# A two-layer hybrid decoder on one core: the MLP norm's factor is squared and applied behind the second product, and ScalarE's Relu reads the up stage's bank

## The chip, the core and the metric

The kernel runs on one core of one Trainium2 chip. The metric is device microseconds of an execution. A core has five engines with queues of their own: TensorE (PE) multiplies matrices into the banks of PSUM; VectorE (DVE), ScalarE (ACT) and GpSimd (POOL) work element by element; SyncE (SP) issues most of the transfers. Each engine executes its queue in order and waits at the head of it for semaphores of the others.

## The reference, cut to what matters

The reference is a decoder of two layers on 256 tokens of width 1024. Layer A has differential attention, layer B block attention; both also attend into a fixed memory. Each layer ends with an MLP of width 4096 behind an RMS norm:

```python
def _rmsnorm(x, g):
    y = xf * lax.rsqrt(jnp.mean(xf * xf, axis=-1, keepdims=True) + EPS)
    return (y * g.astype(jnp.float32)).astype(x.dtype)

def _sq_relu_mlp(h, w_up, w_down):
    u = jax.nn.relu(h @ w_up)
    return (u * u) @ w_down

x = x + _sq_relu_mlp(_rmsnorm(x, a_norm_mlp[i]), a_w_up[i], a_w_down[i])
```

The norm has one positive factor r per token. The up product is linear in it, relu keeps a positive factor, the square squares it, and the down product is linear again: the factor can be taken out of the whole MLP as r squared, which is 1 / (mean + EPS), without a root.

## The kernel before

Every float32 product is made of three products of rounded parts: high by high, low by high, high by low. Of a weight chunk (128x1024) that a transfer brings, ACT makes the high part (L336) and DVE the low part (L338); there are six buffers of each part, four for the raw chunk. Of a normalized activation ACT makes the high part (L352) and DVE the low one (L354); they carry the gain of the norm but not its factor.

An MLP has two stages. The **up stage** (`mlp_up`) has 16 steps, each of two chunks into one bank `acc` of 128x512: 128 hidden units by 256 tokens, twice. Tokens lie along the free axis there, so the factor is needed as a row repeated over all partitions. PE first sums the squares (L460), DVE makes 1 / sqrt of them in eleven small instructions (L466, the lines of `rsqrt`, L468), multiplies the identity by each half's column (L477), PE multiplies this by ones (L479), and DVE copies the result into `rb` (L481). Then DVE reads each bank as max(bank, 0) times `rb` (L790), ACT squares it (L793), ACT and DVE split it into two parts (L805, L807); for six of the 16 steps DVE also makes four block sums (L800 to L803). There are four `acc` banks and two buffers `u`.

The **down stage** (`natural_down`) turns this around: the hidden activations are the weights of PE, and the result has tokens on partitions, in four banks `t` (half of the tokens by half of the columns). Twelve of the 32 row blocks of the down weights go through a scheme of seven products in place of eight; its extra sums go into four `acc` banks `more`, which `gather` folds into the tiles `ys` (first MLP) or `xs` (last MLP, where they hold the residual stream). In the first MLP DVE then adds each bank `t` to its `ys` (L982), PE transposes (L990) and DVE adds the result to `xT` (L751). In `mlp_last` DVE adds the pieces straight into `xs` (L1027, L1045, L1067), then the final norm follows.

The order of the work is not written out by hand. Every step is given to a planner (`Plan`) with an engine, an assumed duration, what it reads and writes and a priority; `order` runs a list schedule on these costs with the buffers' limits, and the instructions are emitted in the order of the planned starts. So a changed step can move others on its engine.

Of the kernel before, what the change touches and what calls it, by code (L numbers as in the profile page):

```python
# [13 lines left out]
AF = mybir.ActivationFunctionType  # L14
# [5 lines left out]
EPS = 1e-6  # L20
# [205 lines left out]
def tile_hybrid(ctx: ExitStack, tc: tile.TileContext, xa, xb, memt, xnat, mnat, w0, wall, consts, fgain, out):  # L226
# [21 lines left out]
    def bank(cls):  # L248
        return buf(cls, [128, 512], F32, psum)
# [8 lines left out]
    def fixed(shape, nm, dt=F32):  # L258
        return const.tile(shape, dt, name=name(nm))
# [11 lines left out]
    nlam = fixed([128, 1], "nlam")  # L271
    rb_t = fixed([128, S], "rb")
    ppx = fixed([128, 2, 512], "ppx")
# [139 lines left out]
    class Stats:  # L413
# [40 lines left out]

        def rstd(self):
            ps = bank("t")
# [7 lines left out]
            def emit():  # L464
# [3 lines left out]
                nc.vector.tensor_scalar_mul(self.r8, self.r, 0.125)  # L468
            P.add(("dve", 2100, emit), [ps], [self.key])
            return self  # L470

    def bcast(st):

        ps = bank("t")
        for h in range(2):
            dg = buf("dg", [128, 128])
            P.add(("dve", 196, lambda dg=dg, h=h: nc.vector.tensor_scalar_mul(dg.t, ident, st.r[:, h:h + 1])),  # L477
                  [st.key], [dg])
            P.add(("pe", 213, lambda dg=dg, h=h: nc.tensor.matmul(  # L479
                ps.t[:, h * 128:(h + 1) * 128], ones, dg.t, start=True, stop=True)), [dg], [ps])  # L480
        P.add(("dve", t_dve(S), lambda: nc.vector.tensor_copy(rb_t, ps.t[:, 0:S])), [ps], ["rb"])  # L481

# [291 lines left out]
    def mlp_up(st, sums=()):  # L774

        st.rstd()
        us = [big(i, [128, 4, 2, S], F32R) for i in range(8)]
        st_["pieces"] = 1
        first = True
        for b in range(16):  # L780
            u = buf("u", [128, 2, S])
            ps = bank("acc")
            for mi in range(2):
                wh, wl = chunk()
                up_chunk(ps, mi, wh, wl)
            if first:
                bcast(st)
                first = False
            k0 = 2 * b % 4
            P.add(("dve", t_dve(512, True), lambda u=u, ps=ps: nc.vector.scalar_tensor_tensor(  # L790
                u.t, ps.t.rearrange("p (a s) -> p a s", a=2), 0.0, rb_t[:, None, :].to_broadcast([128, 2, S]),
                op0=OP.max, op1=OP.mult)), [ps, "rb"], [u])
            P.add(("act", t_act(512), lambda u=u: nc.scalar.activation(u.t, u.t, AF.Square)), [u], [u])  # L793
# [158 lines left out]
    def mlp(st, done):  # L952
# [4 lines left out]
        def gather(more):  # L957
# [8 lines left out]
            add((1, 1), (1, 0), r5)  # L966
            add((0, 1), (0, 1), r5)

        part = 24
        _, product, u_ = natural_down(us, pss, part, part, gather,  # L970
                                      wsum, lambda a: [("wsum", a)], 4)
        for c in range(2):
# [7 lines left out]
            for hf in range(2):  # L980
                y, ps = ys[hf, c], pss[hf, c]
                P.add(("dve", t_dve(512), lambda y=y, ps=ps: nc.vector.tensor_add(y.t, y.t, ps.t)), [y, ps], [y])  # L982
            for b in range(2):
# [14 lines left out]
    def mlp_last(st):  # L998
# [22 lines left out]
        def gather(more):  # L1021
# [7 lines left out]
            def to(cell, src, key, port=False):  # L1029
                x = xs[cell]  # L1030
                add(lambda: x.t, lambda: x.t, src, [(x, 0), (x, 1), key], [(x, 0), (x, 1)], port)
            r1, r5, r6, r7 = more
# [11 lines left out]
        x, ps, tail = xs[1, 1], pss[1, 1], bank("acc")  # L1044
        P.add(("dve", t_dve(S), lambda x=x, ps=ps: nc.vector.tensor_add(x.t[:, S:], x.t[:, S:], ps.t[:, S:])),  # L1045
              [ps, (x, 1)], [(x, 1)])
        for hf in range(2):
            ss, part_, r = fixed([128, 4], "ss"), fixed([128, 1], "part"), fixed([128, 1], "rstd")
            for c in range(2):
# [5 lines left out]
                for i in range(2):  # L1055
# [4 lines left out]
                    if c == 1 and i == 1:  # L1060
# [5 lines left out]
                    dump = buf("sq", [128, S])  # L1066
                    P.add(("dve", t_dve(S), lambda x=x, ps=ps, sl=sl: nc.vector.tensor_add(  # L1067
                        x.t[:, sl], x.t[:, sl], ps.t[:, sl])), [ps, (x, i)], [(x, i)])
                    P.add(("act", t_act(S) + 100, lambda x=x, sl=sl, dump=dump, ss=ss, j=2 * c + i: nc.scalar.activation(
# [332 lines left out]
```

## Time and profile before

| what | value |
|---|---|
| time, median of three runs | 599.97 us (599.6 to 600.78) |
| span of the profiled execution | 725.8 us |
| mean clock granted to TensorE in it | 0.755 |
| PE busy | 716.6 us |
| DVE busy | 491.3 us |
| ACT busy | 398.0 us |
| POOL busy | 54.4 us |
| moved by transfers | 108.45 MB, mean 149 GB/s |

The profiled execution took longer than the timed ones; its page gives the span and no time around it. In the views "<-" behind an idle time names what ended it, and a group's line gives the line of the kernel, the engine, the operation, what it writes and reads, the number of instructions, the busy time and the mean duration. PEld is the loading of PE's weights, which overlaps the products. One product of float32 parts in the source can stand as several records.

### The profile page before, as it was taken

How to read it: one execution, taken by the hardware profiler on the slowest of the kernel's cores; microseconds unless marked ns; L12 is line 12 of the kernel's file. 1: busy time of each engine (PE TensorE's matmuls, PEld its weight loads, DVE VectorE, ACT ScalarE, POOL GpSimd, SP SyncE). 2: the span in 40 equal slices, each digit the busy share in tenths (PEclk: the TensorE clock that was granted, in tenths of full speed). 3: DMA queues.
4: the chain of work that ended last, by engine and by line, in shares of the span. 5: the costliest groups of instructions: out<-in, count | busy, mean ns of one | idle time of the engine just before them, and what ended most of it. 6: DMA issues, size and time to landing. Idle time of an engine off the chain costs nothing.

```text
span 725.8 us, 10368 instructions
## 1 busy us (share of the span) xinstructions
PE 716.6 (99%) x3794; PEld 590.5 (81%) x3794; DVE 491.3 (68%) x871; ACT 398.0 (55%) x750; POOL 54.4 (8%) x67
## 2 busy tenths in 40 slices
PE   9999999999999999999999999999999999999996
PEld 7676769999999977677777776889999999776775
DVE  5777666587556687766776577675675666876664
ACT  6776666455544554444575477656464455554422
POOL 0121110030000000000111121001200000000002
PEclk8777777777777777777777777777777777777777
DMA  8854432435444433546455432224444443354421
GB/s 303 293 183 165 146 95 79 145 119 175 151 168 146 152 139 132 188 145 209 139 174 179 169 120 85 88 88 143 153 164 152 154 158 125 127 186 151 148 85 59
DMA packets 30003, 108.45 MB, mean 149 GB/s; under 512 B 3328, under 2 KB 3328, under 8 KB 29696
## 3 DMA queue, kind: packets, MB, share of 16 engines
q1 hardware_dynamic: 29664, 107.26, 43.4%
q8 instruction: 30, 0.49, 0.3%
q10 hardware_dynamic: 288, 0.52, 0.2%
q14 instruction: 21, 0.17, 0.1%
HBM read 106.72 MB, written 1.05 MB: 148 GB/s over the span
## 4 chain that ended last, share of the span: by engine, by line
PE 98%; DVE 1%; DMA 1%; ACT 0%; issue 0%; SPq 0%; ACTq 0%
PE acc L821 30%; PE acc L499 23%; PE t L871 23%; PE acc L765 7%; PE acc L871 6%; PE t L586 2%; PE t L624 2%; PE t L681 1%; PE t L557 1%; DMA xT<-xa 1%; PE t L1013 0%; PE t L990 0%; DVE xT L751 0%; PE t L579 0%; PE t L721 0%; PE t L720 0%
## 5 line engine op out<-in xcount | busy, mean ns | idle before, releaser
L336 ACT CAST wh<-w 128x512 fp32r<-128x512 f32 (+1 forms) x232 | 182.5, 814 | 191.3 <-PE acc L821 74.0
L338 DVE TENSOR_TENSOR wl<-w,wh 128x512 fp32r<-128x512 f32 (+1 forms) x232 | 213.4, 939 | 86.7 <-ACT wh L336 71.7
L821 PE MATMUL acc<-xn,wh 128*128 128x256 f32 x1024 | 157.3, 314 | 0.5 <-DVE xn L354 0.5
L821 PEld LDWEIGHTS acc<-xn,wh 128*128 128x128 f32 x1024 | 150.7, 224 | 0.7 <-DVE xn L354 0.7
L871 PE MATMUL t<-wh,B 128*128 128x512 f32 (+1 forms) x368 | 134.4, 453 | 0.0
L499 PE MATMUL acc<-wh,xn 128*128 128x512 f32 x256 | 101.6, 472 | 0.7 <-ACT xn L352 0.7
L871 PEld LDWEIGHTS t<-wh,B 128*128 128x128 f32 x368 | 72.5, 199 | 29.8
L821 PE MATMUL acc<-xn,wl 128*128 128x256 f32 x512 | 84.1, 314 | 0.0
L871 PE MATMUL t<-wl,B 128*128 128x512 f32 (+1 forms) x184 | 82.9, 450 | 0.0
L821 PEld LDWEIGHTS acc<-xn,wl 128*128 128x128 f32 x512 | 78.1, 224 | 0.0
L499 PEld LDWEIGHTS acc<-wh,xn 128*128 128x128 f32 x256 | 51.0, 199 | 23.5 <-issue 2.2
L765 PE MATMUL acc<-B,wh 128*128 128x256 f32 x256 | 60.1, 323 | 0.0
L499 PE MATMUL acc<-wl,xn 128*128 128x512 f32 x128 | 58.0, 453 | 0.0
L790 DVE SCALAR_TENSOR_TENSOR u<-acc,rb 128x512 f32<-128x512 f32 x32 | 21.9, 690 | 50.5 <-PE acc L821 50.5
L871 PEld LDWEIGHTS t<-wl,B 128*128 128x128 f32 x184 | 37.0, 201 | 15.1
L765 PEld LDWEIGHTS acc<-B,wh 128*128 128x128 f32 x256 | 46.3, 216 | 0.9 <-issue 0.8
L452 POOL TENSOR_TENSOR sqa<-sqa,sq 128x256 f32<-128x256 f32 x21 | 20.3, 966 | 295.7 <-ACT sq L451 294.9
L765 PE MATMUL acc<-B,wl 128*128 128x256 f32 x128 | 40.0, 313 | 0.0
L895 DVE TENSOR_TENSOR wl<-wsum,wh 128x1024 fp32r<-128x1024 f32 x24 | 29.4, 1223 | 8.9 <-ACT wh L894 6.5
L533 POOL TENSOR_TENSOR ropet<-ropes,consts 128x256 f32<-128x256 f32 (+1 forms) x28 | 25.1, 917 | 129.0 <-ACT ropes L522 106.5
L499 PEld LDWEIGHTS acc<-wl,xn 128*128 128x128 f32 x128 | 26.8, 210 | 9.1
L894 ACT CAST wh<-wsum 128x1024 fp32r<-128x1024 f32 x24 | 25.3, 1052 | 15.9 <-PE acc L871 6.9
(223 smaller groups left out, 899.1 us busy)
## 6 DMA issues: line engine op xcount, KB each, us to landing
w<-wall SPq DMA_DIRECT2D x191, 512.0 KB, 3.3
w<-memt SPq DMA_DIRECT2D x4, 512.0 KB, 5.0
B<-xnat SPq DMA_DIRECT2D x1, 1024.0 KB, 7.4
B<-mnat SPq DMA_DIRECT2D x1, 1024.0 KB, 8.9
xT<-xa SPq DMA_DIRECT2D x1, 540.0 KB, 3.8
w<-w SPq DMA_DIRECT2D x2, 256.0 KB, 3.5
xT<-xb SPq DMA_DIRECT2D x1, 512.0 KB, 6.6
consts<-consts SPq DMA_DIRECT2D x1, 256.5 KB, 4.5
```

The source lines that it names most:

```text
L336: P.add(("act", t_act(n), lambda sl=sl: nc.scalar.copy(h.t[:, sl], w.t[:, sl])), [(w, x) for x in q], [(h, x) for x in q])
L338: P.add(("dve", t_dve(n), lambda sl=sl: nc.vector.tensor_sub(l.t[:, sl], w.t[:, sl], h.t[:, sl].bitcast(F32))), [(w, x) for x in q] + [(h, ...
L452: P.add(("pool", t_pool(S), lambda: nc.gpsimd.tensor_tensor(self.acc.t, self.acc.t, sq.t, op=OP.add)), [sq, self.acc], [self.acc])
L499: nc.tensor.matmul(pss[hf].t[:, c0:c1], a(k)[:, ts], b.t[:, o + c0:o + c1], start=(k == 0 and i == 0), stop=(k == KT - 1 and i == 2))
L533: nc.gpsimd.tensor_tensor(t.t[:, 0:nh, e:e + 32], zs.t[:, 0:nh, 32 - e:64 - e], b(sin[:, e:e + 32]), op=OP.mult)
L586: nc.tensor.matmul(sp[hd].t[:, c], qk[a].t[r, qb * 128:(qb + 1) * 128], qk[b].t[r, S:S + c.stop - c.start], start=(qb == 0 and i == 0 and ...
L765: nc.tensor.matmul(o, a.t[:, ws], x(k), start=(n == 0 and m % 2 == 0 and i == 0), stop=(n == KT - 1 and i == 2), skip_group_check=True)
L790: P.add(("dve", t_dve(512, True), lambda u=u, ps=ps: nc.vector.scalar_tensor_tensor(u.t, ps.t.rearrange("p (a s) -> p a s", a=2), 0.0, rb_ ...
L821: nc.tensor.matmul(ps.t[:, o], w.t[:, k * 128:(k + 1) * 128], xnt[:, k, x], skip_group_check=True, **flags)
L871: nc.tensor.matmul(ps.t[:, c0:c1], x, y, start=start and i == 0, stop=stop and i == 2, skip_group_check=True)
L894: P.add(("act", t_act(m), lambda: nc.scalar.copy(h[x].t[:, :m], src())), keys, [h[x]])
L895: P.add(("dve", t_dve(m), lambda: nc.vector.tensor_sub(l[x].t[:, :m], src(), h[x].t[:, :m].bitcast(F32))), keys + [h[x]], [l[x]], port=True)
```

## The change

The factor is no longer applied to the up stage's bank. `rstd(True)` makes r squared with two instructions, a multiply-add and a reciprocal; `bcast` and `rb` are gone. ACT reads the bank with Relu. Behind the down product the factor is a column, one number per token's partition: in the first MLP ACT scales the four gathered `ys`, and DVE's sum of bank and `ys` becomes a multiply-add; in the last MLP each sum into the residual tiles becomes a multiply-add with the column.

```diff
-        def rstd(self):
+        def rstd(self, squared=False):
...
-            P.add(("dve", 2100, emit), [ps], [self.key])
+            def square():
+                ms = fixed([128, 2], "ms")
+                nc.vector.tensor_scalar(ms, ps.t[:, 0:2], 1.0 / D, EPS, op0=OP.mult, op1=OP.add)
+                nc.vector.reciprocal(self.r, ms)
+            P.add(("dve", 350, square) if squared else ("dve", 2100, emit), [ps], [self.key])
...
-    def bcast(st):
-        ps = bank("t")
-        for h in range(2):
-            dg = buf("dg", [128, 128])
-            P.add(("dve", 196, lambda dg=dg, h=h: nc.vector.tensor_scalar_mul(dg.t, ident, st.r[:, h:h + 1])),
-                  [st.key], [dg])
-            P.add(("pe", 213, lambda dg=dg, h=h: nc.tensor.matmul(
-                ps.t[:, h * 128:(h + 1) * 128], ones, dg.t, start=True, stop=True)), [dg], [ps])
-        P.add(("dve", t_dve(S), lambda: nc.vector.tensor_copy(rb_t, ps.t[:, 0:S])), [ps], ["rb"])
...
     def mlp_up(st, sums=()):
-        st.rstd()
+        st.rstd(True)
...
-            P.add(("dve", t_dve(512, True), lambda u=u, ps=ps: nc.vector.scalar_tensor_tensor(
-                u.t, ps.t.rearrange("p (a s) -> p a s", a=2), 0.0, rb_t[:, None, :].to_broadcast([128, 2, S]),
-                op0=OP.max, op1=OP.mult)), [ps, "rb"], [u])
+            P.add(("act", t_act(512, True), lambda u=u, ps=ps: nc.scalar.activation(
+                u.t, ps.t.rearrange("p (a s) -> p a s", a=2), AF.Relu)), [ps], [u])
...
             add((0, 1), (0, 1), r5)
+            for (hf, c), y in ys.items():
+                P.add(("act", t_act(512, False, True), lambda y=y, hf=hf: nc.scalar.activation(
+                    y.t, y.t, AF.Copy, scale=st.r[:, hf:hf + 1])), [y, st.key], [y])
...
-                P.add(("dve", t_dve(512), lambda y=y, ps=ps: nc.vector.tensor_add(y.t, y.t, ps.t)), [y, ps], [y])
+                P.add(("dve", t_dve(512), lambda y=y, ps=ps, hf=hf: nc.vector.scalar_tensor_tensor(
+                    y.t, ps.t, st.r[:, hf:hf + 1], y.t, op0=OP.mult, op1=OP.add)), [y, ps, st.key], [y])
...
-                add(lambda: x.t, lambda: x.t, src, [(x, 0), (x, 1), key], [(x, 0), (x, 1)], port)
+                P.add(("dve", t_dve(512), lambda: nc.vector.scalar_tensor_tensor(
+                    x.t, src(), st.r[:, cell[0]:cell[0] + 1], x.t, op0=OP.mult, op1=OP.add)),
+                    [(x, 0), (x, 1), key, st.key], [(x, 0), (x, 1)], port=port)
...
-                    P.add(("dve", t_dve(S), lambda x=x, ps=ps, sl=sl: nc.vector.tensor_add(
-                        x.t[:, sl], x.t[:, sl], ps.t[:, sl])), [ps, (x, i)], [(x, i)])
+                    P.add(("dve", t_dve(S), lambda x=x, ps=ps, sl=sl, hf=hf: nc.vector.scalar_tensor_tensor(
+                        x.t[:, sl], ps.t[:, sl], st.r[:, hf:hf + 1], x.t[:, sl], op0=OP.mult, op1=OP.add)),
+                        [ps, (x, i), st.key], [(x, i)])
```

The step at L1045 is changed in the same way. The planner makes a new order of this. SP's and POOL's rows stand as before. On PE the only difference in the whole program is four rows. The place is the start of the first MLP's up stage, before; `acc_...` are banks, `xn` the activations, `wh` and `wl` the parts of a chunk, `sqa` the sums of squares, `dg` the diagonals:

```order
L460 MATMUL t_1742<-ones_116,sqa_1596 128x1 x2
L821 MATMUL acc_1615<-xn_67,wl_1515 128x256 x4
L821 MATMUL acc_1615<-xn_67,wh_1538 128x256 x16
L821 MATMUL acc_1615<-xn_67,wl_1546 128x256 x8
L821 MATMUL acc_1625<-xn_67,wh_1568 128x256 x2
L821 MATMUL acc_1625<-xn_67,wl_1635 128x256 x8
L479 MATMUL t_1813<-dg_1805,ones_116 128x128
L479 MATMUL t_1813<-dg_1807,ones_116 128x128
L821 MATMUL acc_1625<-xn_67,wh_1612 128x256 x16
```

The same place after the change, where the line of `up_chunk` is L809:

```order
L460 MATMUL t_1741<-ones_115,sqa_1595 128x1 x2
L809 MATMUL acc_1614<-xn_67,wl_1514 128x256 x4
L809 MATMUL acc_1614<-xn_67,wh_1537 128x256 x16
L809 MATMUL acc_1614<-xn_67,wl_1545 128x256 x8
L809 MATMUL acc_1624<-xn_67,wh_1567 128x256 x2
L809 MATMUL acc_1624<-xn_67,wl_1634 128x256 x8
L809 MATMUL acc_1624<-xn_67,wh_1611 128x256 x16
```

The two rows L479 are gone and nothing else has moved; the second MLP's up stage loses its two in the same way.

On ACT the same up stage begins like this before (L336 casts a chunk, L793 squares, L805 makes the high part):

```order
L336 CAST wh_1724<-w_1560 128x1024
L336 CAST wh_1738<-w_1641 128x1024
L336 CAST wh_1785<-w_1707 128x1024
L336 CAST wh_1799<-w_1730 128x1024
L336 CAST wh_1841<-w_1767 128x1024
L793 ACTIVATE u_1843<-u_1843 128x512
L805 CAST B_394_1867<-u_1843 128x2x256
L793 ACTIVATE u_1854<-u_1854 128x512
L805 CAST B_394_1867<-u_1854 128x2x256
```

And after (L335 is the cast of a chunk, L779 the Relu, L781 the square, L793 the high part):

```order
L335 CAST wh_1723<-w_1559 128x1024
L779 ACTIVATE u_1737<-acc_1598 128x512
L335 CAST wh_1744<-w_1640 128x1024
L781 ACTIVATE u_1737<-u_1737 128x512
L793 CAST B_377_1768<-u_1737 128x2x256
L335 CAST wh_1783<-w_1706 128x1024
L779 ACTIVATE u_1795<-acc_1614 128x512
L335 CAST wh_1803<-w_1729 128x1024
L781 ACTIVATE u_1795<-u_1795 128x512
L793 CAST B_377_1768<-u_1795 128x2x256
```

The first bank is read before four of the casts that used to stand ahead of its square, and a Relu that waits for PE stands in front of casts.

Near the end of the first MLP's down stage ACT's order is this before (L963 copies the first gathered sum, L352 makes parts of the memory's activations):

```order
L963 COPY qh_3221<-acc_2799 128x512
L336 CAST wh_3228<-w_3173 128x1024
L336 CAST wh_3233<-w_3185 128x1024
L336 CAST wh_3245<-w_3211 128x1024
L336 CAST wh_3269<-w_3235 128x1024
L336 CAST wh_3283<-w_3252 128x1024
L336 CAST wh_3304<-w_3264 128x1024
L352 ACTIVATE wh_3324<-w_3281,xT_66 128x256 x4
```

And after (L951 is that copy, L957 scales one of the four tiles `ys`):

```order
L951 COPY qh_3201<-acc_2780 128x512
L335 CAST wh_3208<-w_3153 128x1024
L335 CAST wh_3213<-w_3165 128x1024
L335 CAST wh_3225<-w_3191 128x1024
L957 ACTIVATE qh_3201<-qh_3201,rstd_134 128x512
L335 CAST wh_3250<-w_3215 128x1024
L335 CAST wh_3264<-w_3232 128x1024
L957 ACTIVATE qh_3243<-qh_3243,rstd_134 128x512
L957 ACTIVATE ql_3227<-ql_3227,rstd_134 128x512
L957 ACTIVATE ql_3257<-ql_3257,rstd_134 128x512
L335 CAST wh_3288<-w_3245 128x1024
L351 ACTIVATE wh_3308<-w_3262,xT_66 128x256 x4
```

The casts keep their sequence; one scaling stands after the third of them and three ahead of the last.

More of the change, by code (lines that the diff above doesn't have):

```diff
@@ L271, in tile_hybrid @@
     nlam = fixed([128, 1], "nlam")
-    rb_t = fixed([128, S], "rb")
     ppx = fixed([128, 2, 512], "ppx")
@@ L774, in mlp_up @@
     def mlp_up(st, sums=()):
-        st.rstd()
+        st.rstd(True)
         us = [big(i, [128, 4, 2, S], F32R) for i in range(8)]
         st_["pieces"] = 1
-        first = True
         for b in range(16):
@@ L785, in mlp_up @@
                 up_chunk(ps, mi, wh, wl)
-            if first:
-                bcast(st)
-                first = False
             k0 = 2 * b % 4
-            P.add(("dve", t_dve(512, True), lambda u=u, ps=ps: nc.vector.scalar_tensor_tensor(
-                u.t, ps.t.rearrange("p (a s) -> p a s", a=2), 0.0, rb_t[:, None, :].to_broadcast([128, 2, S]),
-                op0=OP.max, op1=OP.mult)), [ps, "rb"], [u])
+            P.add(("act", t_act(512, True), lambda u=u, ps=ps: nc.scalar.activation(
+                u.t, ps.t.rearrange("p (a s) -> p a s", a=2), AF.Relu)), [ps], [u])
             P.add(("act", t_act(512), lambda u=u: nc.scalar.activation(u.t, u.t, AF.Square)), [u], [u])
@@ L1044, in mlp_last @@
         x, ps, tail = xs[1, 1], pss[1, 1], bank("acc")
-        P.add(("dve", t_dve(S), lambda x=x, ps=ps: nc.vector.tensor_add(x.t[:, S:], x.t[:, S:], ps.t[:, S:])),
-              [ps, (x, 1)], [(x, 1)])
+        P.add(("dve", t_dve(S), lambda x=x, ps=ps: nc.vector.scalar_tensor_tensor(
+            x.t[:, S:], ps.t[:, S:], st.r[:, 1:2], x.t[:, S:], op0=OP.mult, op1=OP.add)),
+            [ps, (x, 1), st.key], [(x, 1)])
         for hf in range(2):
```

## The prediction

> **What bounds the kernel now.** I read the page first (busy shares, granted clock, chain shares), then who TensorE waited for, then the busy time by stage, and last the chain at the places the change touches. From the page:
>
> ```profile
> span 725.8 us, 10368 instructions
> ...
> PE 716.6 (99%) x3794; PEld 590.5 (81%) x3794; DVE 491.3 (68%) x871; ACT 398.0 (55%) x750; POOL 54.4 (8%) x67
> ...
> PEclk8777777777777777777777777777777777777777
> ...
> PE 98%; DVE 1%; DMA 1%; ACT 0%; issue 0%; SPq 0%; ACTq 0%
> ```
>
> And from the view of the cores:
>
> ```profile
> core 0: 725.8 us, clock 0.755
> ```
>
> TensorE (PE) is busy in 716.6 of 725.8 us, and the chain that ended last is PE for 98% of the span. A busy PE alone proves little; the waits decide. This is all that PE waited for:
>
> ```profile
> PE wu L287 <- DVE ones_b L284: 1.1, 1, 1.1
> PE acc L499 <- ACT xn L352: 0.7, 1, 0.7
> PE acc L821 <- DVE xn L354: 0.5, 1, 0.5
> ```
>
> 2.3 us in the whole span, all three before the code that changes. So in this execution a microsecond taken off PE's queue is a microsecond off the span, and work moved between VectorE (DVE) and ScalarE (ACT) is worth nothing as long as neither makes PE wait.
>
> One caution comes with every number below. The timed runs have a median of 599.97 us, the profiled execution has a span of 725.8 us; the page gives no time around the span. The ratio is 0.827. If all of it is clock, the 0.755 that the profile granted on average becomes 0.913 in the timed runs (my estimate); the page cannot show it. PE's share then shrinks against the other engines, so I look at how close they are. The stages, in the order PE, PEld, DVE, ACT, POOL after the window's length; the first is the up stage of the first MLP, the next two its passage into the down stage, the last two the same passage in the second MLP:
>
> ```profile
> 165.50:257.50 92.00, 92.00 (x649) 91.95 (x649) 59.78 (x88) 46.65 (x58) 0.00 (x0) 0.75 0.47 155
> 257.40:269.30 11.90, 11.90 (x44) 8.30 (x43) 10.23 (x13) 7.82 (x11) 0.00 (x0) 0.75 0.31 103
> 269.33:282.08 12.75, 12.75 (x46) 8.94 (x46) 10.25 (x12) 6.35 (x7) 0.00 (x0) 0.75 0.45 161
> 615.00:627.00 12.00, 12.00 (x44) 8.53 (x43) 9.82 (x13) 7.88 (x12) 0.00 (x0) 0.75 0.28 102
> 627.00:639.70 12.70, 12.70 (x46) 8.95 (x45) 10.65 (x13) 6.32 (x7) 0.00 (x0) 0.75 0.44 154
> ```
>
> In the up stage DVE fills 59.78 of 92.00 us and ACT 46.65. At the passage DVE is at 86%: near enough to matter at a higher clock, not at this one.
>
> **The change part by part.** *Removed from PE: the broadcast.* The rows L479 go from both MLPs; the rest of PE's order stands as it was. The chain around them:
>
> ```profile
> 158.98 0.43 PE t L460 x4
> 159.41 5.51 PE acc L821 x38
> 164.92 0.55 PE t L479 x4
> 165.47 4.55 PE acc L821 x32
> ...
> 522.53 0.57 PE t L479 x4
> ```
>
> 0.55 + 0.57 = 1.12 us of PE, with PE busy on both sides. Nothing hides it, and nothing moves into the hole: the next matmuls (L821) stand ready. In the timed runs it is 1.12 x 0.827 = 0.93 us.
>
> *Removed from DVE: the root chain, the two diagonals, the copy of the broadcast.* Eleven small instructions become two and three more vanish, none of them anything that PE waits for in the list above. Cover: PE's 5.51 us of L821 between the statistics and L479. Gain in the span: 0. After this the first bank's reader waits for PE's bank alone, so its release comes earlier; PE never waited for that release.
>
> *Moved: 32 readings of a bank, DVE to ACT.* What one costs, what stands nearest to the Relu, and how the engines wait:
>
> ```profile
> L790 DVE SCALAR_TENSOR_TENSOR u<-acc,rb x32: 681/692/693, 167.0 to 615.1; 128x512 f32<-128x512 f32 x32
> ...
> L560 ACT COPY qh<-t x5: 567/587/588, 46.2 to 88.9; 128x512 f32<-128x512 f32 x5
> ...
> L793 ACT ACTIVATE u<-u 128x512 f32<-128x512 f32 x32 | 20.2, 633 | 21.1 <-DVE u L790 21.1
> ...
> ACT wh L336 <- PE acc L821: 74.0, 55, 2.9
> ...
> DVE u L790 <- PE acc L821: 50.5, 26, 2.1
> ```
>
> No Relu from PSUM is in the trace; the copy of a 128x512 bank by ACT (587 ns) is the same shape, so I take 0.59 us, with the Square's 633 ns as upper end. ACT gains 16 x 0.59 = 9.4 us per up stage, 46.65 becomes 56 of 92.00; DVE falls from 59.78 to about 48.7. The Relu now waits for PE's bank in ACT's queue, and behind it stand Square, copy and the casts of later weight chunks (L336). Those casts already wait for PE, 74.0 us over 55 waits, 1.35 us each: the buffers are all full, six chunks ahead. A chunk is 24 matmuls of 92.00 / 649 = 0.142 us, 3.4 us, so the lead is 20 us against 0.59. Cost 0; range 0 to the price of the slower rival below.
>
> The Trainium skill, "ScalarE: Activation LUTs", section "Rules for kernel authors", speaks against this move: relu belongs on VectorE, which it calls up to about three times faster per element (said of bf16). For this fp32 bank the rows disagree: 692 ns on DVE, 587 ns for a plain read on ACT. The rule taken at its largest would be an estimate of 2.1 us per Relu; what that would do is the second form of rival C.
>
> *Added to ACT in the first MLP's down stage: four scalings of the partial sums y.* Their neighbours on ACT and the price of a scaling:
>
> ```profile
> L1100 ACT ACTIVATE qh<-qh,rstd x1: 618/618/618, 712.3 to 712.3; 128x384 f32<-128x384 f32 x1
> ...
> 333.75 1.06 ACT L336 CAST wh<-w 128x1024 fp32r<-128x1024 f32 x1 [0.65 <-PE t L871]
> 337.16 1.05 ACT L336 CAST wh<-w 128x1024 fp32r<-128x1024 f32 x1 [2.35 <-PE t L871]
> 340.55 1.05 ACT L336 CAST wh<-w 128x1024 fp32r<-128x1024 f32 x1 [2.34 <-PE t L871]
> ```
>
> 384 columns cost 618 ns, so 512 some 0.72 us. One stands before the cast at 333.75, three before that at 340.55: 2.2 us into a wait of 2.34 us. Cost 0; if the wait were gone, at most 2.9 us of ACT behind six buffered chunks, still nothing at PE. The later sum into y (L982) reads the scaled y, but waits for PE's last product, at 346.82 and later (below).
>
> *Changed on DVE: additions become multiply-adds with a per-row factor.* Price and the one place where it shows:
>
> ```profile
> L354 DVE SCALAR_TENSOR_TENSOR B<-t,consts,B x6: 478/484/485, 94.8 to 138.4; 128x256 fp32r<-128x256 f32 x6
> ...
> L1067 DVE TENSOR_TENSOR ql<-ql,acc x1: 422/422/422, 718.9 to 718.9; 128x256 f32<-128x256 f32 x1
> ...
> 346.82 0.69 DVE L982 TENSOR_TENSOR qh<-qh,t 128x512 f32<-128x512 f32 x1 [0.63 <-PE t L871]
> 347.67 0.69 DVE L982 TENSOR_TENSOR qh<-qh,t 128x512 f32<-128x512 f32 x1 [0.16 <-PE t L871]
> ...
> 349.33 1.12 PE t L990 x8
> ...
> 716.32 2.56 PE acc L871 x18
> 718.88 0.02 issue
> 718.91 0.43 DVE ql L1067
> 719.34 0.02 issue
> ```
>
> A 128x256 multiply-add on a bank with a column of factors takes 484 ns, the addition 422: +0.06 us each, 19 times in all. Eighteen have slack: the first MLP's second sum (L982) ends at 348.36, 1 us before PE reaches the transposes (L990) that read it, and those of the last MLP run while PE is still in L871. The last one, at 718.91, is on the path behind PE's last matmul: +0.06 us. Bounds: 0 to +0.1.
>
> **The sum.** In the profiled execution -1.12 + 0.06 = -1.06, 725.8 to 724.7. In the timed runs -0.93 + 0.06 = -0.87, 599.97 to 599.1. That is 0.15%, under the 0.2% that a measurement of this kernel can tell from no change (the three runs shown lie from 599.6 to 600.78).
>
> **The rivals.** *A, relief of DVE: clearly faster.* At full clock the four passage windows need 11.90 x 0.75 = 8.93, 9.56, 9.00 and 9.53 us of PE against 10.23, 10.25, 9.82 and 10.65 of DVE. DVE is late by 1.30 + 0.69 + 0.82 + 1.12 = 3.9 us, and four readings per MLP near these windows (4 x 0.69 = 2.8 us) leave DVE. Gain at most 3.9 on top: 595.2; half of it 597.1. It decides above a clock of 11.90 x 0.75 / 10.23 = 0.87, and my estimate for the timed runs is 0.913. Against it: even at that clock DVE has a fifth of the up stage free (59.78 of 92.00 x 0.827 = 76.1 us) and is six chunks ahead, which covers a deficit of 1 to 2 us per MLP. The Trainium skill, "TensorE: Matmul & The Clock Gate", Part 1, says that one or two busy cores never trip the current limiter; by that rule the single core here would run at full clock and A would be live. The trace, 0.75 on one core, disagrees for the profiled execution.
>
> *B, absorbed: no change.* If the timed runs have waits of PE behind the up stage that this trace doesn't have (a late DVE in the down stage, say, that A's relief does not reach), PE arrives 0.93 us early and waits it out: 600.0. For it: 0.827 may not be all clock. Against it: no such wait in the trace.
>
> *C, slower: ACT's queue at the passage.* In the last three banks of each up stage ACT carries Relu, Square and copy and also the casts of the first down chunks. If its lead has gone, each Relu delays the cast behind it by its full 0.59 us and PE stands: 3 x 0.59 x 2 = 3.5 us, 599.1 + 3.5 = 602.6. It decides where ACT's busy time passes PE's: 7.82 + 0.59 = 8.4 us in the window at 257.40 against 11.90 x 0.827 = 9.8 in the timed runs, or 8.93 at full clock. It is short of that in each case, so it needs a wait that ACT's queue adds. Its second form is a slow Relu: at three times L790, 2.1 us, ACT would need 46.65 + 16 x 2.1 = 80 us for the up stage against 76.1 in the timed runs, 4 us late per MLP, 607; the copy's 587 ns speaks against it.
>
> That the change does not do what it says is excluded on PE: the order shows the L479 rows gone.
>
> **How the numbers follow.** Forecast (PE-bound, -0.87): 0.60. A: 0.20. B: 0.12. C: 0.08, of which 0.01 for its second form. The forecast's own range is 598.3 to 599.6, since PE may at a higher clock reach L479 before the DVE chain is done, a wait that would also go. Of its 0.60 I give 0.22 to a reading beyond 0.2% (below 598.8) and 0.38 to one within. Faster: 0.22 + 0.19 of A = 0.41. Same: 0.38 + 0.12 of B + 0.01 = 0.51. Slower: 0.08. The range 596.0 to 600.6 takes in the forecast, B and more than half of A; it leaves out C and A's far end.
>
> **What would show it.** Right: no L479, PE still waits under 3 us in all, DVE's busy time in the up stage near 49 us and ACT's near 56 in 92, the last L1067 near 484 ns, the span shorter by about 1 us. Wrong: a wait of PE at L821 or L871 for a cast (C); a span shorter by several us at the same clock (A); a Relu far above 0.63 us.

## The result and the profile after

The changed kernel takes 604.92 us (median of four executions, 604.07 to 605.94), the kernel before on the same chip 599.79 us (598.34 to 600.78): ratio 1.0102, 95% interval 1.0071 to 1.0133. It is slower by 1.0%, where 599.1 us was forecast and 600.6 was the upper end. Three slow executions are left out of the ratios of this document: 605.48 us in e12, 973.73 in e14 at a granted clock of 0.559, and one of 3315.84 of the kernel before beside e8 to e11.

The page and the view of the cores of the kernel after:

```profile
span 602.2 us, 10298 instructions
PE 590.7 (98%) x3786; PEld 520.1 (86%) x3786; DVE 466.8 (78%) x815; ACT 410.2 (68%) x786; POOL 56.2 (9%) x67
PE 87%; DMA 4%; DVE 4%; ACT 3%; issue 1%; SPq 0%; ACTq 0%
core 0: 602.2 us, clock 0.998
```

The profile before had a clock of 0.755 and can't be laid beside this one. So the first experiment was the kernel before once more, for a profile at the same clock. Its page:

```profile
span 595.4 us, 10368 instructions
PE 583.9 (98%) x3794; PEld 514.8 (86%) x3794; DVE 485.9 (82%) x871; ACT 390.3 (66%) x750; POOL 56.1 (9%) x67
```

PE has eight records fewer (the L479 products) and is busy for 6.8 us more; the span is longer by the same 6.8 us. The medians above differ by 5.1 only: the executions of the kernel before beside them, 598.34 to 600.78 us, were slower than the profiled one (597.2), and no trace of them is kept. What PE waited for, after:

```profile
PE acc L809 <- DVE xn L353: 1.1, 1, 1.1
PE wu L286 <- DVE ones_b L283: 1.1, 1, 1.1
PE acc L492 <- ACT xn L351: 1.0, 1, 1.0
PE acc L492 <- DVE wl L337: 0.5, 2, 0.2
PE acc L492 <- ACT wh L335: 0.4, 1, 0.4
PE t L572 <- ACT qh L553: 0.3, 1, 0.3
```

4.4 us in all, and none of it is a wait for the Relu or for the work behind it. The kernel before at the same clock waited 4.2 us:

```profile
PE acc L821 <- DVE xn L354: 1.1, 1, 1.1
PE wu L287 <- DVE ones_b L284: 1.1, 1, 1.1
PE acc L499 <- ACT xn L352: 0.9, 1, 0.9
PE acc L499 <- DVE wl L338: 0.6, 2, 0.4
PE t L624 <- ACT B L703: 0.5, 1, 0.5
```

So the time isn't in a wait. It is in the products themselves. The groups of products of the up stage (L821 before, L809 after) and of L499 (L492 after) that read xn, with their busy us and mean ns, before and then after:

```profile
L821 PE MATMUL acc<-xn,wh 128*128 128x256 f32 x1024 | 128.2, 277 | 1.1 <-DVE xn L354 1.1
L821 PE MATMUL acc<-xn,wl 128*128 128x256 f32 x512 | 69.1, 277 | 0.0
...
L499 PE MATMUL acc<-wh,xn 128*128 128x512 f32 x256 | 86.2, 405 | 1.0 <-ACT xn L352 0.9
L499 PE MATMUL acc<-wl,xn 128*128 128x512 f32 x128 | 51.1, 399 | 0.2 <-DVE wl L338 0.2
```

```profile
L809 PE MATMUL acc<-xn,wh 128*128 128x256 f32 x1024 | 132.2, 280 | 1.1 <-DVE xn L353 1.1
L809 PE MATMUL acc<-xn,wl 128*128 128x256 f32 x512 | 71.1, 280 | 0.0
...
L492 PE MATMUL acc<-wh,xn 128*128 128x512 f32 x256 | 86.9, 407 | 1.0 <-ACT xn L351 1.0
L492 PE MATMUL acc<-wl,xn 128*128 128x512 f32 x128 | 51.2, 400 | 0.2 <-DVE wl L337 0.2
```

The same 1536 products, whose order and sizes the change doesn't touch, take 203.3 us in place of 197.3: 6.0 of the 6.8 us. The 384 products of L492 and xn add 0.8 us (86.9 + 51.2 against 86.2 + 51.1). That is no more than these products differ by in runs that leave them alone (135.7 us in e7 and 137.3 in e8, below), so I don't count it as an effect of the change.

Mean durations of overlapping products say little, so I count them in a fixed stretch. The two windows lie in the middle of the first and of the second up stage; after the length stand PE's busy time and its number of products. Before and then after:

```profile
150.00:210.00 60.00, 60.00 (x532) 60.00 (x531) 47.05 (x70) 36.27 (x46) 0.00 (x0) 1.00 0.58 194
440.00:500.00 60.00, 60.00 (x532) 60.00 (x531) 47.09 (x70) 36.22 (x46) 0.00 (x0) 1.00 0.58 196
```

```profile
150.00:210.00 60.00, 60.00 (x512) 60.00 (x511) 39.76 (x57) 40.60 (x55) 0.00 (x0) 1.00 0.56 187
440.00:500.00 60.00, 60.00 (x511) 60.00 (x511) 38.27 (x54) 39.84 (x52) 0.00 (x0) 1.00 0.55 185
```

532 products of 128x256 against 512 in 60 us at the same clock, with PE busy all the time in both: 112.8 and 117.2 ns a product. (The counts take in products that the window's edges cut. By the chain of the whole stretch, 648 products take 73.45 us before and 686 take 80.90 after, 113.3 and 117.9 each, with nearly the same difference.) I call these the short and the long pitch. 4.4 ns times 1536 would be 6.8 us; 6.0 show, since some products ran at the long pitch before as well. The question for the experiments is what sets the pitch.

One more view gives the hint: the chain of work of the kernel before, from the statistics products (L460) of the first MLP up to 147 us, where both views end, and the same place after:

```profile
136.67 0.34 PE t L460 x4
137.00 4.58 PE acc L821 x38
141.59 0.44 PE t L479 x4
142.03 5.00 PE acc L821 x44
```

```profile
136.57 0.34 PE t L460 x4
136.91 10.12 PE acc L809 x85
```

Before, 38 products behind L460 take 4.58 us, 120.5 ns each; 44 behind L479 take 5.00, 113.6 each. After, the 85 behind L460 take 119.1 each, and there is no L479 any more.

### The profile page after: what moved, and what is told of

The parts are those of the page before. It is cut to its first block, busy times and chain, and to the rows that moved or that the text cites. A ratio compares the mean times of both kernels' runs of the same rounds, so it can differ in the third digit from the quotient of the medians.

```text
span 602.2 us, 10298 instructions
## 1 busy us (share of the span) xinstructions
PE 590.7 (98%) x3786; PEld 520.1 (86%) x3786; DVE 466.8 (78%) x815; ACT 410.2 (68%) x786; POOL 56.2 (9%) x67
## 4 chain that ended last, share of the span: by engine, by line
PE 87%; DMA 4%; DVE 4%; ACT 3%; issue 1%; SPq 0%; ACTq 0%
PE acc L809 30%; PE t L859 22%; PE acc L492 15%; PE acc L758 7%; PE acc L859 6%; PE t L579 2%; PE t L617 2%; DVE wl L337 2%; PE t L674 1%; DMA B<-xnat 1%; DMA w<-wall 1%; DMA w<-memt 1%; ACT wh L335 1%; PE t L550 1%; DMA xT<-xa 1%
## 5 line engine op out<-in xcount | busy, mean ns | idle before, releaser
L335 ACT CAST wh<-w 128x512 fp32r<-128x512 f32 (+1 forms) x232 | 182.5, 815 | 119.3 <-PE acc L809 45.4
L809 PE MATMUL acc<-xn,wh 128*128 128x256 f32 x1024 | 132.2, 280 | 1.1 <-DVE xn L353 1.1
L809 PEld LDWEIGHTS acc<-xn,wh 128*128 128x128 f32 x1024 | 125.5, 188 | 1.5 <-DVE xn L353 1.3
L859 PE MATMUL t<-wh,B 128*128 128x512 f32 (+1 forms) x368 | 112.1, 386 | 0.0
L492 PE MATMUL acc<-wh,xn 128*128 128x512 f32 x256 | 86.9, 407 | 1.0 <-ACT xn L351 1.0
L859 PE MATMUL t<-wl,B 128*128 128x512 f32 (+1 forms) x184 | 71.1, 387 | 0.0
L809 PE MATMUL acc<-xn,wl 128*128 128x256 f32 x512 | 71.1, 280 | 0.0
L809 PEld LDWEIGHTS acc<-xn,wl 128*128 128x128 f32 x512 | 64.9, 188 | 0.0
L492 PEld LDWEIGHTS acc<-wh,xn 128*128 128x128 f32 x256 | 48.8, 191 | 14.5 <-issue 1.4
L492 PE MATMUL acc<-wl,xn 128*128 128x512 f32 x128 | 51.2, 400 | 0.2 <-DVE wl L337 0.2
L758 PE MATMUL acc<-B,wh 128*128 128x256 f32 x256 | 50.8, 289 | 0.0
L598 ACT ACTIVATE B<-t,nm 128x128 f32<-128x128 f32 (+1 forms) x64 | 27.0, 438 | 4.6 <-DVE nm L594 2.5
L492 PEld LDWEIGHTS acc<-wl,xn 128*128 128x128 f32 x128 | 24.5, 192 | 5.6 <-DVE wl L337 0.5
```

Of the source, the lines that this page charges most:

```text
L335: P.add(("act", t_act(n), lambda sl=sl: nc.scalar.copy(h.t[:, sl], w.t[:, sl])), [(w, x) for x in q], [(h, x) for x in q])
L492: nc.tensor.matmul(pss[hf].t[:, c0:c1], a(k)[:, ts], b.t[:, o + c0:o + c1], start=(k == 0 and i == 0), stop=(k == KT - 1 and i == 2))
L598: nc.scalar.activation(p[hd].t[:, c], sp[hd].t[:, c], AF.Exp, bias=nm[hd][:, qb:qb + 1], accum_out=ss[:, hd, qb:qb + 1])
L758: nc.tensor.matmul(o, a.t[:, ws], x(k), start=(n == 0 and m % 2 == 0 and i == 0), stop=(n == KT - 1 and i == 2), skip_group_check=True)
L809: nc.tensor.matmul(ps.t[:, o], w.t[:, k * 128:(k + 1) * 128], xnt[:, k, x], skip_group_check=True, **flags)
L859: nc.tensor.matmul(ps.t[:, c0:c1], x, y, start=start and i == 0, stop=stop and i == 2, skip_group_check=True)
```

## The experiments

First theory (theory 1 of the expectations): the Relu on ACT reads the bank in another way or at another time, or holds up ACT's queue, and PE pays for it. Its rivals: the place of the tiles in SBUF (theory 2, later A), which moves because `rb` (1024 bytes per partition) and some small tiles are gone; the transfers of the opening (theory 3); and, from e8 on, the missing L479 (theory P). Theories B and Q of the expectations put the loss down to the change's own work, whichever engine does it. The expectations call the weight buffers the ring. The edits are cut to the lines that matter; from e8 on each but that of e9 has unused bytes behind xn too, 128 as in e7, 64 in e11 and 192 in e15.

All ratios are to runs of the kernel before on the same chip. The table gathers the runs; "distance" is the byte address of the first weight buffer less that of xn, both in SBUF per partition, modulo 256 (every weight buffer and every part of xn lies a multiple of 256 bytes further on, so it is the same for each product of the up stage). Modulo 512 the four distances are 64, 448, 0 and 128, so no run tells whether the pattern repeats every 256 bytes or every 512. The two counts are PE's products in the two 60 us windows; the row "before" has those of e1.

| run | distance | where the two L479 stood | products, 1st and 2nd MLP | ratio (95%) |
|---|---|---|---|---|
| before | 64 | L479 | 532, 532 | 1 |
| after | 192 | none | 512, 511 | 1.0102 (1.0071 to 1.0133) |
| e2 | 192 | none | 512, 512 | 1.0116 (1.0094 to 1.0138) |
| e3 | 192 | none | 512, 512 | 1.0114 (1.0093 to 1.0135) |
| e4 | 64 | none | 512, 512 | 1.0084 (1.0068 to 1.0099) |
| e5 | 192 | L479 | 511, 512 | 1.0147 (1.0124 to 1.0170) |
| e6 | 192 | none | 512, 512 | 1.0117 (1.0100 to 1.0135) |
| e7 | 64 | none | 511, 511 | 1.0077 (1.0058 to 1.0096) |
| e8 | 64 | two unread products | 532, 531 | 0.9992 (0.9979 to 1.0005) |
| e9 | 192 | two unread products | 512, 512 | 1.0127 (1.0110 to 1.0143) |
| e10 | 64 | one, behind L460 | 532, 532 | 1.0005 (0.9987 to 1.0023) |
| e11 | 0 | one, behind L460 | 503, 502 | 1.0140 (1.0126 to 1.0154) |
| e12 | 64 | none; L460 widened | 512, 512 | 1.0040 (1.0013 to 1.0067) |
| e13 | 64 | two, behind L460 | 532, 512 | 1.0029 (1.0001 to 1.0058) |
| e14 | 64 | two of one column | 512, 532 | 1.0072 (1.0040 to 1.0104) |
| e15 | 128 | two unread products | 502, 508 | 1.0148 (1.0110 to 1.0187) |

**e1, the kernel before, once.** No edit.

> The kernel before, unchanged, for a profile at the clock of the timed runs (the changed kernel's profile has 0.998 and a span of 602.2). All theories expect a span near 598. Theory 1 (ACT's queue: Relu in front of squares and casts) expects the 4 to 5 us between the two to lie in the two up stages and the passages behind them: in the changed kernel the first up stage runs from 128.9 to 217.8 and the second from 418.4 to 511.4. Theory 2 (the tile rb, 1 KB per partition, is gone and every later tile has another address) expects the difference to be spread over stages that the change doesn't touch. Theory 3 (transfers of the opening) expects it before 95 us.

Measured: 597.2 us, span 595.4 at a clock of 0.998. Its rows stand above: they are what the profile after is compared with from here on. Theory 3 falls with it: the first product of the up stage starts at 129.23 us in e1 and at 128.89 after, so the opening loses nothing.

**e2, the changed kernel with `rb` kept,** unread. It was meant to keep the weight buffers where they were and came within 128 bytes of that.

```diff
+    rb_t = fixed([128, S], "rb")
+    nc.vector.memset(rb_t[:, 0:1], 0.0)
```

> The changed kernel with the tile rb still allocated and one column of it written once at the start, so that later tiles keep the addresses they had before. Theory 1 (ACT's queue): 605, as the changed kernel. Theory 2 (addresses): 600 or a little under, 599.1 if the prediction's sum holds. Theory 3 (opening transfers): 605 unless the addresses steer them.

Measured: 604.24 us, 1.0116. The kilobyte alone changes nothing. The weight buffers then begin at byte 75040 and not at 75168 as before, 128 short, since four small tiles of the root chains are gone too, so this run doesn't test their place.

**e3, the same bank read by DVE,** a max with 0 in place of the Relu.

```diff
-            P.add(("act", t_act(512, True), lambda u=u, ps=ps: nc.scalar.activation(
-                u.t, ps.t.rearrange("p (a s) -> p a s", a=2), AF.Relu)), [ps], [u])
+            P.add(("dve", t_dve(512), lambda u=u, ps=ps: nc.vector.tensor_scalar_max(
+                u.t, ps.t.rearrange("p (a s) -> p a s", a=2), 0.0)), [ps], [u])
```

> The changed kernel, but DVE reads the up stage's bank with a maximum against 0, and ACT no longer does; the factor stays behind the second product and there is no broadcast. Theory 1 (ACT's queue): 599, the loss is gone since ACT's queue is as before but for the four scalings. Theory 2 (addresses): 605. Theory 3 (opening transfers): 605.

Measured: 604.45 us, 1.0114, 512 products in each window. The engine that reads the bank makes no difference. The first theory falls; the rivals are left.

**e4, the changed kernel with 1152 unused bytes** in place of the tiles that went, so that every weight buffer lies where it lay before.

```diff
+    pad_t = fixed([128, 288], "pad")
+    nc.vector.memset(pad_t[:, 0:1], 0.0)
```

> The changed kernel with an unused tile of 1152 bytes per partition, one column of it written once at the start, so that the ring of the weight buffers begins at byte 75168 of a partition again, as in the kernel before, and not at 74016; the tile xn stays at 24928. Theory A (place: PE's products that read xn run at 115 ns a piece or at 118, by where the weight buffers lie against xn): ratio to before 0.9985, up-stage matmuls with a median of 276 ns as before. Theory B (the change's own work in the up stage disturbs PE, whoever reads the bank): ratio 1.010, median 279 as in the changed kernel.

Measured: 601.87 us, 1.0084. A part comes back, not the whole. In the trace the first products of each up stage now run at the short pitch (113 ns from start to start), up to the statistics products L460; behind them all run at 118 ns to the end of the stage.

**e5, the kernel before with its weight buffers 128 bytes lower,** by sharing two pairs of small scratch tiles. Each engine's order of instructions is that of before.

```diff
+        k = 1 if n == 2 and len(shared[n][0]) >= 3 else None
+        t, q = (shared[n][0][k], shared[n][1][k]) if k else (fixed([128, n], "rst"), fixed([128, n], "rsq"))
```

> The kernel before with the same order of instructions on every engine; only the temporaries of two root chains are shared with an earlier one, so that the ring begins 128 bytes lower, at 75040, as it did in the run with rb kept. Theory A (place): ratio 1.010, up-stage matmuls at 279 ns. Theory B (the change's own work): ratio 1.000, 276 ns.

Measured: 605.01 us, 1.0147. The kernel before, with nothing changed but places, loses 1.5%, more than the 1.0% that theory A expected. Its windows:

```profile
150.00:210.00 60.00, 60.00 (x511) 60.00 (x511) 45.20 (x67) 35.65 (x45) 0.00 (x0) 1.00 0.55 185
440.00:500.00 60.00, 60.00 (x512) 60.00 (x511) 46.25 (x71) 35.78 (x46) 0.00 (x0) 1.00 0.59 192
```

DVE is as busy as in the kernel before (45 to 46 us against 47), PE is never idle, and it is at the long pitch although L479 is there. So the place alone does it.

**e6 and e7, 128 unused bytes** ahead of xn or behind it. Both put the weight buffers at byte 74144; in e6 xn moves with them, in e7 it stays.

```diff
+    pad_t = fixed([128, 32], "pad")
+    nc.vector.memset(pad_t[:, 0:1], 0.0)
```

> The changed kernel with an unused tile of 128 bytes ahead of xn: xn moves from 24928 to 25056 and the ring from 74016 to 74144, so their distance stays 49088. Theory A in the form that the distance between xn and the ring matters: ratio 1.009, 279 ns. Theory A in the form that the ring's own address modulo 256 matters: 0.9985, 276 ns. Theory B: 1.010.

> The changed kernel with the unused tile of 128 bytes behind xn: xn stays at 24928, the ring begins at 74144, 1024 bytes below its place in the kernel before. Theory A in the form that only the place modulo 256 counts: ratio 0.9985, 276 ns. Theory A in the form that the exact place counts: anything up to 1.010. Theory B: 1.010.

Measured: e6 604.32 us, 1.0117, as without the bytes; e7 601.51 us, 1.0077, as e4 with its 1152. It isn't the address of the buffers that counts but their distance from xn; and since e4 and e7 lie 1024 bytes apart and behave alike, only a rest of that distance counts, which I give modulo 256. What e4 and e7 still lack beside the kernel before shows behind L460, where both go over to the long pitch. In the profiles only 0.5 us of what e7 gains over e6 lies in the up stages (L811 takes 202.9 us against 203.4); 2.9 us lie in the products of L494 (135.7 against 138.6), and since e8 at the same distance has 137.3 there, no run shows that this part belongs to the distance.

**e8, the changed kernel at distance 64 with two products that nobody reads,** fp32 and 128x128, at the first bank of each up stage, near where L479 stood (12 products behind L460, where L479 had 38 ahead of it in the first MLP). **e9,** the same at the changed kernel's own distance.

```diff
+            if b == 0:
+                dead = bank("t")
+                for h in range(2):
+                    P.add(("pe", 213, lambda h=h: nc.tensor.matmul(
+                        dead.t[:, h * 128:(h + 1) * 128], ones, ident, start=True, stop=True)), [st.key], [dead])
```

> Changed kernel with 128 unused bytes behind xn (the distance between xn and the ring of buffers is then that of the kernel before, modulo 256) and with two fp32 128x128 products, which nobody reads, set into TensorE's queue at the first bank of each up stage, where the two broadcast products stood. Theory P (the broadcast products put TensorE back to the short pitch of 113.5 ns that the one-column statistics products had ended): pitch about 118 ns only between the statistics products and the dead ones, 113.5 ns behind; some 4.5 ns x 1440 matmuls = 6 us less than the same kernel without the dead products (ratio 1.0077), plus 0.9 us for the dead products themselves: ratio 0.998 to 1.001. Theory Q (the time is lost to the Relu, the added multiplies or something else in the change): 0.9 us longer than without, ratio 1.009.

> Changed kernel at its own place (192 modulo 256) with the same two unread fp32 128x128 products. If place and products are two separate causes and the place alone holds TensorE at the long pitch, the products bring nothing back: pitch 117 to 118 ns throughout, ratio 1.010 to 1.013. If the products alone were enough: pitch 113.5 ns behind them and ratio 1.000.

Measured: e8 596.56 us, 0.9992; e9 604.52 us, 1.0127. The chain of e8 around the added products (L783; L816 is the up stage):

```profile
136.18 0.34 PE t L462 x4
136.52 1.52 PE acc L816 x12
138.04 0.45 PE t L783 x4
138.48 11.57 PE acc L816 x102
```

and its windows:

```profile
150.00:210.00 60.00, 60.00 (x532) 60.00 (x531) 40.51 (x58) 41.06 (x56) 0.00 (x0) 1.00 0.61 194
440.00:500.00 60.00, 60.00 (x531) 60.00 (x531) 40.51 (x58) 41.06 (x56) 0.00 (x0) 1.00 0.60 193
```

Behind the unread products 102 of the up stage take 11.57 us, 113.4 ns each. Work without any use, 0.9 us of it, makes the kernel 5 us faster than e7, and all of the change's own work is still there, so theory Q falls. In e9 the same products bring back nothing. Behind that place these profiles have the short pitch with the distance of 64 and the two products together (e1, e8), and not with the products alone (e5, e9) or the distance alone (e4, e7).

The distance of 192 doesn't shut the short pitch out, though. Ahead of L460 the up stage has an uninterrupted stretch of 63 products in the first MLP and one of 70 in the second. The kernel after and then e3, both at 192:

```profile
128.89 7.69 PE acc L809 x63
421.36 8.52 PE acc L809 x70
```

```profile
130.05 7.41 PE acc L809 x63
422.24 8.26 PE acc L809 x70
```

e3 has the times of the kernels at 64 there (e1: 7.43 and 8.28), and so has the stretch of 70 in e2 and in e9 (8.26 each). Behind L460 all of them are at the long pitch. So the distance shifts which pitch an interruption leaves behind; it doesn't fix it.

**e10, one such product directly behind the statistics; e11,** the same at distance 0 (64 unused bytes in place of 128).

```diff
+            if squared:
+                dead = bank("t")
+                P.add(("pe", 213, lambda: nc.tensor.matmul(
+                    dead.t[:, 0:128], ones, ident, start=True, stop=True)), [self.acc], [dead])
```

> Changed kernel at the good place (128 unused bytes behind xn) with one unread fp32 128x128 product directly behind the statistics products of each MLP. If one such product is enough to put TensorE back: pitch 113.5 ns at once behind it, and the shortest time of all kernels so far, ratio 0.997 to 0.999 (0.45 us less product time and some 0.3 us less of the long pitch than with two later on). If it takes the state that two products or the later place leave: pitch stays 118 ns, ratio 1.008.

> As the one with one product directly behind the statistics products, but 64 unused bytes in place of 128, which makes the distance between xn and the ring 0 modulo 256. If only 192 is bad: as that one, 113.5 ns and 0.997 to 0.999. If the distance that was tuned by chance (64) is the only good one: 117 to 118 ns from the start of the stage and a ratio of 1.010 or more.

Measured: e10 597.34 us, 1.0005, but with executions from 595.64 to 600.81, where those of e8 lie from 595.79 to 597.75. The ratio lies above the 0.997 to 0.999 that was expected. Its profiled one (span 594.0, the shortest of all profiles) has the short pitch in both MLPs; 3 us more is what one MLP at the long pitch costs (768 x 4.4 ns = 3.4 us, an estimate; the executions of 598 us and more have no trace). e11 605.6 us, 1.0140, with 503 and 502 products in the windows: at distance 0 the long pitch is longer still.

**e12, no added product; the statistics products 128 columns wide** (the same sum 128 times) at distance 64.

```diff
+                    w = 128 if squared else 1
+                    nc.tensor.matmul(ps.t[:, h * w:(h + 1) * w], self.acc.t[:, h * 128:(h + 1) * 128], ones[:, 0:w],
```

> Changed kernel at the good place (128 unused bytes behind xn), no unread product; in each MLP the two statistics products are 128 columns wide (the same sum 128 times over) in place of one column. If the one-column product is what throws TensorE out of the short pitch: 113.5 ns right through both up stages, PE busy 582 to 583 us, ratio 0.997 to 1.001, some 6 us less than the same kernel with one-column products (1.0077). If it is any change between fp32 and the rest that does it, or the statistics' own wait: 118 ns behind them, ratio 1.008.

Measured: 601.44 us, 1.0040, executions from 596.21 to 602.39; the profiled one shows the long pitch from L460 on in both MLPs. Neither side of the expectation fits all executions: the one column is not what throws PE out, or not alone.

**e13, two wide unread products directly behind the statistics; e14, two of one column** where those of e8 stood. The edit is that of e14 against e8; e13 has e8's two products in e10's place.

```diff
-                        dead.t[:, h * 128:(h + 1) * 128], ones, ident, start=True, stop=True)), [st.key], [dead])
+                        dead.t[:, h:h + 1], ident, ones[:, 0:1], start=h == 0, stop=True, skip_group_check=True)), [st.key], [dead])
```

> Changed kernel at the good place with two unread fp32 128x128 products directly behind the statistics products of each MLP (the run with one there had executions from 595.6 to 600.8 us). If the wide pair is what puts TensorE back each time: executions close together, 595 to 597.5 us, pitch 113.5 ns behind it in both MLPs, ratio 0.998 to 1.000. If the pitch behind an interruption is a matter of chance: executions spread over 595 to 602 us again.

> Changed kernel at the good place with two unread products of one column (stationary the identity, fp32) where the two 128-column ones stood in the run with ratio 0.9992. If any interruption lets TensorE fall back into the short pitch: ratio 0.998 to 1.001. If the one-column product is what throws it out and the width of the last products decides: pitch 118 ns to the end of both up stages, ratio 1.007 to 1.009. If it is chance: executions from 595 to 602 us.

Measured: e13 599.87 us, 1.0029, executions from 596.6 to 604.69; e14 1.0072, executions from 599.5 to 604.91. The windows of e13 and then of e14:

```profile
150.00:210.00 60.00, 60.00 (x532) 60.00 (x531) 40.43 (x57) 40.90 (x55) 0.00 (x0) 1.00 0.58 194
440.00:500.00 60.00, 60.00 (x512) 60.00 (x511) 38.82 (x55) 41.25 (x55) 0.00 (x0) 1.00 0.56 185
```

```profile
150.00:210.00 60.00, 60.00 (x512) 60.00 (x511) 39.75 (x57) 40.19 (x54) 0.00 (x0) 1.00 0.57 186
440.00:500.00 60.00, 60.00 (x532) 60.00 (x531) 40.87 (x58) 40.91 (x55) 0.00 (x0) 1.00 0.59 195
```

One execution holds both pitches: in e13 the first MLP has the short one and the second the long one, in e14 the other way round, with the same instructions in both MLPs. So the pitch can change at each interruption of the run of equal products, and then holds to the next. Wide or narrow, one or two, an interruption can leave either. With its two products there, e8 seems to have fallen into the short pitch in each of its 11 executions: their times lie within 2 us of one another, and one MLP at the long pitch would add 3.4. On the same chip e10, with one product and directly behind L460, spreads over 5 us. So the place or the number shifts the odds; these runs don't separate the two. The kernel before isn't safe from it either: beside e8 its executions end at 598.5 us, but beside e13 and e15, on two other chips, single ones reach 602.06 and 602.08 at granted clocks of 0.997 and 0.999. An MLP at the long pitch would explain them; no trace of them is kept.

**e15, e8 at distance 128** (192 unused bytes).

```diff
-    pad_t = fixed([128, 32], "pad")
+    pad_t = fixed([128, 48], "pad")
```

> The kernel of ratio 0.9992 (two unread fp32 products at the first bank of each up stage) with 192 unused bytes behind xn in place of 128: the distance between xn and the ring is then 128 modulo 256, the one class of 64-byte steps not yet run. If 64 is the only good distance: 512 products or fewer in 60 us of the up stage and a ratio of 1.012 to 1.015, as at 0 and 192. If the bad ones are 0 and 192, those next to a multiple of 256 on its lower side: 532 products in 60 us and 0.998 to 1.001.

Measured: 607.0 us, 1.0148, 502 and 508 products in the windows. Of the four distances that were tried, only 64, that of the kernel before, let PE run the bulk of an up stage at the short pitch in any profile.

No version beats both kernels by more than a measurement can tell; e8 comes nearest (0.9992, 0.9979 to 1.0005).

## Why the prediction was wrong, point by point

**The step that failed** is the first term, "Nothing hides it, and nothing moves into the hole: the next matmuls (L821) stand ready", together with "a microsecond taken off PE's queue is a microsecond off the span". It gave L479 its own price and took the price of every other product as fixed. The removed rows were worth what I said: 0.44 us in the first MLP by the chain at full clock, twice that for both, 0.88 against my 0.93. But the 1536 products of the up stages have two prices, 112.8 and 117.2 ns, and the change took away both things that kept most of them at the lower one: the two L479 that put PE back behind L460 (e8 against e7), and the distance of 64 between xn and the weight buffers (e5, where nothing else changes). 6.0 us more in L809 and 0.9 less for L479 make 5.1; the span grew by 6.8, and the rest, 0.8 of it in L492, is spread over groups that no run here ties to the change.

Losing either one is enough for the long pitch behind L460 in these profiles: e7 keeps the distance and loses the products, e9 keeps the products and loses the distance. Undoing one of them therefore gains little (e7 601.51 us against the 604.32 of e6 on the same chip, e9 nothing), which looked like "not the cause" until both were undone.

**Could the profile before have shown it?** Not at its clock: there 92.00 us held 649 products, 141.8 ns each, and both pitches measured at full clock lie below that. The 38 products behind L460 took 5.51 us there, 0.12 more than at that pace; the interruption alone costs about as much at full clock (10.12 us for 85 after, 0.10 more than at 117.9 ns), so they show no second pitch. The kernel before at full clock does show it, in 4.58 us for 38 products ahead of L479 and 5.00 for 44 behind.

**The clock.** I read 0.827, the timed median over the profiled span, as a clock of 0.913. The kernel before has a span of 595.4 us at 0.998. A product doesn't scale with the clock alone: 141.8 x 0.755 / 0.998 would be 107.3 ns, the short pitch is 112.8. The Trainium skill, "TensorE: Matmul & The Clock Gate", Part 1, says that one or two busy cores never trip the current limiter; every later profile of this one core agrees (0.993 to 0.998), the first one with 0.755 doesn't, and no run here shows why. One execution of e14 without a profile doesn't either (0.559).

**DVE and ACT: right but for one figure.** The groups after of the Relu and of two of the four scalings:

```profile
L779 ACT ACTIVATE u<-acc 128x512 f32<-128x512 f32 x32 | 18.9, 592 | 0.0
L957 ACT ACTIVATE qh<-qh,rstd 128x512 f32<-128x512 f32 x2 | 1.4, 721 | 0.0
```

The last multiply-add in the chain after, behind PE's last product, and the addition in its place in the kernel before at full clock:

```profile
593.09 2.17 PE acc L859 x18
595.26 0.02 issue
595.28 0.50 DVE ql L1062
```

```profile
586.39 2.17 PE acc L871 x18
588.56 0.02 issue
588.58 0.43 DVE ql L1067
```

The Relu takes 592 ns (0.59 forecast), a scaling 721 (0.72), the last multiply-add 0.50 us against 0.43 for the addition before (+0.07, forecast +0.06). DVE is busy 19.1 us less (485.9 to 466.8), ACT 19.9 us more (390.3 to 410.2), and PE waits for neither behind the up stage. In the stretch of the first up stage that I had forecast at 49 us of DVE and 56 of ACT (648 products, 141.6 to 217.6 us) they are busy for 50.1 and 51.3: the first is right, the second 5 us too high.

**The rivals.** A (relief of DVE) had its condition, a clock above 0.87, and still no gain: the kernel before at 0.998 has no wait of PE at the passage that relief could end, so the six buffered chunks cover DVE's deficit, as argued against it. B and C needed waits that neither list has; C's sign came true by another road. That the change leaves PE's other products alone, which the order says and which I took for a proof about time, is true of their order and not of their pace. 0.08 for slower was too little, since all of it hung on waits.

**The list of what would show it** named waits, busy times, the Relu and the span. The missing L479, the busy time of DVE and the last L1067 (484 ns) came out as "right". PE's waits are 4.4 us, not under 3, but they were 4.2 before; and the span is not 1 us shorter but 6.8 longer. None of its signs of "wrong" came: no wait for a cast in the up or down stage, no shorter span, no slow Relu. It had no line for the pace of PE's unchanged products, which is where the 1% went.

## What to carry to other kernels

Where PE is busy all the time, compare the number of its products per microsecond in a stage, not only its waits and its share: here 6.0 of the 6.8 us lost were in products that the change didn't touch. A removed tile or a removed product can move the rest's addresses and rhythm; before such an edit is judged, put an unused tile of the same size, and if need be an unread product, in its place and measure what is left, over several executions, since one execution can hold both pitches. A distance in SBUF between the two operands of a long run of products is a setting like any other, worth trying in steps of 64 bytes.

## What the hardware showed

Runs of equal fp32r products (128x128 weights, 256 columns), all with weight load and product overlapped and PE never idle, went at one of two paces at the same clock in these runs: 112.8 or 117.2 ns at distances of 64 and 192 bytes modulo 256 between the operands. At distance 0 it was 119.3 (60 us by 503), at 128 it was 119.5 and 118.1 (502 and 508). At 64 the pace changed at interruptions by fp32 products, of 1 or of 128 columns, and then held for hundreds of products. At 192 all products behind L460 ran at the long pitch in every profile, and some stretches ahead of it at the short one (e2, e3, e9). Why the distance matters, why 64 is the good one, and what about an interruption decides its outcome stay open.
